# Attention with bias on one core: five landing places instead of four, fewer E tiles and output buffers, and a new written-out order

## The chip, the core and the metric

The kernel runs on one core of a Trainium2 chip. The metric is the device time of one execution in microseconds; the median of several executions counts. A profile is one more execution, taken apart by the hardware profiler: its span is the time from the first to the last instruction of the program, and the execution's own time stands beside it.

The engines of the core are called TensorE (PE: matrix products; its weight loads are PEld), VectorE (DVE), ScalarE (ACT), GpSimd (POOL) and SyncE (SP, which only issues DMAs here).

## The reference

Four batches of eight heads, 1024 queries and keys of 64 numbers each, and one bias matrix for all heads:

```python
batch, n_heads, seq_len, head_dim = 4, 8, 1024, 64
scale = 1.0 / np.sqrt(head_dim)
scores = scale * np.matmul(q, k.transpose(0, 1, 3, 2))
scores = scores + bias                       # bias is (1, 1, 1024, 1024)
scores_max = np.max(scores, axis=-1, keepdims=True)
attn = np.exp(scores - scores_max) / (np.sum(np.exp(scores - scores_max), axis=-1, keepdims=True) + 1e-8)
return np.matmul(attn, v).astype(np.float32)
```

All arrays are float32. The kernel leaves the maximum out, since the scores are small.

## The kernel before

**Work.** The 32 heads are taken as 16 pairs. The 1024 queries of a head are cut into 8 chunks of 128, which gives 256 *slots*, one for each head and chunk. A slot's scores are 128 x 1024 numbers, transposed (keys on the partitions). They lie in two of six PSUM banks, so three slots fit (`pl`, three lanes of two banks). The slots run in two groups of 9 and 7 pairs (`GROUPS`); the first slot of each chunk in a lane adds the bias through TensorE, and a later one in the lane is made from the scores that still stand there: one product over 128 rows adds the new head's scores and subtracts those of the head before (arrays `ke`, `qe` for even heads, `ko`, `qo` for odd ones). From slot 54 on, two slots of neighbouring chunks are a couple and are filled with products of 256 columns.

**Order.** The whole program is a list of tokens, `ORDER` (line 17), which `do` (line 607) turns into instructions one after the other. Each engine runs its own instructions in the order of the list; across engines only data and buffers order them. The tokens:

- `F12`, `G12`: TensorE fills the first and the second bank of slot 12 (line 376, and line 373 with the bias).
- `X12`: ScalarE takes exp of both banks of slot 12 into two halves of the ring `E` of 28 halves (line 399). `P` and `Q` split a round of three slots into two exps of three banks.
- `f r s h c l` with a slot number: VectorE makes the exp of that slot itself, in six steps (`d_steps`): `f` (fixed point, reads PSUM and so frees the banks), `r` (claims an *E tile* of VectorE, from the pool `de`, which also takes the landing of V), `s`, `h`, `c`, `l`. 29 of the 256 slots go this way.
- `A12`: eight products of slot 12's weights with V and a column of ones (line 462). A letter `a` or `b` opens a new bank of products in one of two further PSUM banks, which the transposes `T` use too. `SIZES` tells how many slots a bank takes.
- `R3`, `M3`: VectorE's reciprocal of bank 3's sums, and its evacuation, a multiplication into an output buffer `ob` of the pool `op`, followed by the stores of that bank (line 664). `joined` (line 465) puts neighbouring chunks of a head, and equal runs of neighbouring heads, into one store; the stores go through SyncE's queue but for the last.
- `Tk5a`, `Ck5`, `Dk5p0`, `Sk5`, `Nq9`, `V3`: transposes of pair 5's k on TensorE (in PSUM bank `a`), their copy out, the doubling of rows for the even head, a copy that sets the two heads side by side ahead of the transposes, negation of q, and the copy of V to its place, all on VectorE but `T`. From pair 2 on, the rows of k for the next pair's even head are copied by a DMA on SyncE's queue (line 603), from pair 9 on all rows for even heads, and those of q.
- `U`, `L`: one further piece of the loads of `LOADS` (line 564) is asked for; it is issued by GpSimd. With `L` it also waits for the last VectorE instruction ahead of it in the list ("issued beside VectorE's long steps").

**Loads.** `more` (line 583) hands out the pieces in their fixed order. The first 27 entries of `LOADS` are always allowed. Those behind them, the *late loads* from k9 on, are allowed once the pair `LANDS` before has given its landing place free (for V: once all products of the pair nine before are made). Each piece also waits until an earlier one has landed, so that only so many are under way: `BEHIND` lists how many for the first pieces, and behind that a constant holds. k and q land in the pool `land`, with `LANDS` places for each.

## Time and profile before

| | before |
|---|---|
| three timed runs | 223.55, 224.82, 225.61 us; median 224.82 us |
| profiled execution | 223.97 us, its span 222.2 us |
| TensorE, weight loads | 214.5 us (97%), 197.5 us (89%) |
| ScalarE | 211.6 us (95%) |
| VectorE | 203.6 us (92%) |
| GpSimd | 72.0 us (32%) |
| granted TensorE clock | full in all slices |

How to read the lines shown below. A line of a group names the kernel line, the engine, the operation, what it writes and reads (`out<-in`) with partitions x elements, and the count; behind the bar stand the busy time in us, the mean duration of one in ns, and the engine's idle time just before them with what ended it. A line of the timeline has the start in us, the duration in us, and the instructions merged into it; in square brackets stands the idle time before it. A line that begins with an operation and three numbers gives the shortest, median and longest duration in ns, and the first and last start in us. "DMA to landing" is the time from issue to landing in us. A line of windows gives the stretch, its length and each engine's busy time with its count (PE, PEld, DVE, ACT, POOL), the granted clock, the DMA engines' share and GB/s.

### The profile page before, as it was taken

The numbers are of one execution on the slowest core, as the hardware profiler recorded it, in microseconds if no ns is written. First come the engines' busy times: TensorE is split into PE (matmuls) and PEld (weight loads), VectorE is DVE, ScalarE is ACT, GpSimd is POOL, SyncE is SP. The second block draws the span as 40 slices with busy tenths as digits, with TensorE's granted clock in tenths as the row PEclk, the third lists the DMA queues.
The fourth block names the chain that finished last, engine by engine and source line by source line (L and its number), as shares of the span: only waits on it lengthen the run. The fifth ranks groups of instructions, "written<-read, shape, count | busy, mean of one in ns | idle before, by whom it ended". The sixth has DMA issues, their size and how long they took to land.

```text
span 222.2 us, 9043 instructions
## 1 busy us (share of the span) xinstructions
PE 214.5 (97%) x3965; PEld 197.5 (89%) x3965; DVE 203.6 (92%) x354; ACT 211.6 (95%) x229; POOL 72.0 (32%) x90
## 2 busy tenths in 40 slices
PE   7799999999999999999999999999999999999993
PEld 2689999999999999999998998898988999899992
DVE  2679999999999999999999999989998999999993
ACT  2799999999999999999999999999999999999992
POOL 8824446637464563030635675410000000000000
PEclk9999999999999999999999999999999999999999
DMA  6999999999999999297899999992111112011213
GB/s 174 227 205 216 227 236 146 173 168 190 128 169 164 88 119 166 62 91 176 102 227 204 215 144 190 119 194 57 44 43 33 55 45 66 7 44 44 86 46 106
DMA packets 86327, 28.87 MB, mean 130 GB/s; under 512 B 66384, under 2 KB 83024, under 8 KB 86288
## 3 DMA queue, kind: packets, MB, share of 16 engines
q0 software_dynamic: 62880, 14.06, 69.9%
q1 hardware_dynamic: 22704, 13.44, 22.6%
q10 hardware_dynamic: 704, 0.79, 1.3%
q8 instruction: 31, 0.51, 1.0%
q14 instruction: 8, 0.07, 0.1%
HBM read 29.36 MB, written 8.39 MB: 170 GB/s over the span
## 4 chain that ended last, share of the span: by engine, by line
ACT 78%; PE 17%; DMA 2%; DVE 1%; issue 0%; SPq 0%; DVEq 0%
ACT E L399 78%; PE pl L376 9%; PE po L462 4%; DMA dy<-in_k_dram 2%; PE px L276 2%; PE pl L373 1%; PE px L282 0%; DVE ob L85 0%; DVE de L85 0%; SPq L501 0%; DVE ko L85 0%; PE pl L276 0%; DVE rs L85 0%; DVEq L85 0%
## 5 line engine op out<-in xcount | busy, mean ns | idle before, releaser
L399 ACT ACTIVATE E<-pl 128x1024 bf16<-128x1024 f32 (+2 forms) x225 | 208.7, 1110 | 1.7 <-PE pl L376 1.6
L462 PE MATMUL po<-vall,E 128*128 128x65 bf16 x1816 | 86.9, 194 | 0.4 <-DVE ob L85 0.2
L462 PEld LDWEIGHTS <-E 128*128 128x128 bf16 x1816 | 77.3, 98 | 3.0 <-DVE ob L85 0.4
L376 PE MATMUL pl<-qo,ko 128*128 128x128 bf16 (+1 forms) x752 | 77.9, 239 | 0.6
L376 PE MATMUL pl<-qe,ke 128*128 128x128 bf16 (+1 forms) x648 | 67.2, 239 | 0.5 <-DVE qe L85 0.2
L376 PEld LDWEIGHTS <-ko 128*128 128x128 bf16 x856 | 57.4, 98 | 6.0 <-ACT E L399 2.1
L376 PEld LDWEIGHTS <-ke 128*128 128x128 bf16 x648 | 43.4, 98 | 5.1 <-ACT E L399 2.2
L85 DVE TENSOR_SCALAR dy<-pl 128x1024 int32<-128x1024 f32 x29 | 35.4, 1221 | 3.7 <-PE pl L376 3.4
L85 DVE SCALAR_TENSOR_TENSOR de<-dy,ds 128x1024 uint16<-128x1024 int32 x29 | 35.1, 1217 | 0.2
L213 POOL DMA_DIRECT2D q<-in_q_dram x18 | 16.6, 921 | 23.8 <-DVE de L85 8.8
L213 POOL DMA_DIRECT2D k<-in_k_dram x18 | 15.9, 887 | 24.1 <-DVE q L85 10.2
L85 DVE TENSOR_TENSOR ob<-po,rs 128x448 f32<-128x448 f32 (+3 forms) x38 | 22.7, 600 | 0.4
L250 POOL DMA_DIRECT2D vall<-in_v_dram x18 | 17.9, 996 | 11.9 <-DVE de L85 4.2
L85 DVE TENSOR_SCALAR de<-dy 128x1024 f16<-128x1024 uint16 x29 | 19.8, 695 | 0.1
L85 DVE TENSOR_TENSOR ds<-de 128x1024 f16<-128x1024 f16 x29 | 19.5, 674 | 0.2
L85 DVE TENSOR_TENSOR ds<-ds,de 128x1024 f16<-128x1024 f16 x29 | 19.5, 679 | 0.0
L373 PE MATMUL pl<-ident,braw 128*128 128x128 bf16 x136 | 14.0, 227 | 0.0
L85 DVE TENSOR_SCALAR qo<-px,sgn 128x1024 bf16<-128x1024 bf16 (+2 forms) x18 | 12.3, 684 | 0.7 <-PE px L276 0.7
L85 DVE TENSOR_SCALAR de<-de 128x1024 f16<-128x1024 f16 x29 | 12.6, 444 | 0.1
L462 PE MATMUL po<-vall,de 128*128 128x65 bf16 x232 | 12.5, 194 | 0.0
L373 PEld LDWEIGHTS <-braw 128*128 128x128 bf16 x136 | 11.8, 148 | 0.4
L85 DVE COPY ko<-px 128x1024 bf16<-128x1024 bf16 (+1 forms) x16 | 10.7, 669 | 1.0 <-PE px L282 1.0
(54 smaller groups left out, 126.0 us busy)
## 6 DMA issues: line engine op xcount, KB each, us to landing
ke<-ko SPq DMA_DIRECT2D x20, 128.0 KB, 4.7
k<-in_k_dram POOLq DMA_DIRECT2D x18, 128.0 KB, 5.3
q<-in_q_dram POOLq DMA_DIRECT2D x18, 128.0 KB, 4.8
out_dram<-ob SPq DMA_DIRECT2D x24, 96.0 KB, 2.8
vall<-in_v_dram POOLq DMA_DIRECT2D x18, 128.0 KB, 6.0
out_dram<-ob SPq DMA_DIRECT2D x30, 64.0 KB, 2.2
braw<-in_bias_dram POOLq DMA_DIRECT2D x7, 256.0 KB, 6.2
de<-in_v_dram POOLq DMA_DIRECT2D x7, 256.0 KB, 7.5
```

Of the source, the lines that this page charges most:

```text
L85: i = getattr(self.engine, name)(*args, **kwargs)
L213: return nc.gpsimd.dma_start(out=t[:, :, y, :], in_=(qf, kf)[x][pr][:, y].rearrange("p (c d) -> p c d", d=D))
L250: return nc.gpsimd.dma_start(out=vall[:, (2 * pr + t) % VR, :, :D], in_=vf[pr][:, t])
L276: m = nc.tensor.transpose(px[:, c, :], raws[pr, which, c0][:, c].rearrange("p t d -> p (t d)"), ident[:])
L373: m = nc.tensor.matmul(to, braw[:, c1, :].rearrange("p (kp kc) -> p kc kp", kc=NCH)[:, kc, :], ident8[:], start=i == 0 and order[0] == "b" ...
L376: m = nc.tensor.matmul(pl[:, 2 * x + b, i * P:(i + n) * P], kk[:, kc, :], qq[:, c:c + n, :].rearrange("p c q -> p (c q)"), start=i == 0 an ...
L399: read(nc.scalar.activation(E[:, e0:e0 + n].rearrange("p b x -> p (b x)"), pl[:, b0:b0 + n].rearrange("p b x -> p (b x)"), ACTF.Exp, scale ...
L462: nc.tensor.matmul(bank[b][:, banks[b].index(s), :], weights(s, kc), vall[:, slots[s][2] % VR, kc, :], start=first and kc == 0, stop=kc == ...
```

## The change

The number of landing places for k and for q goes from four to five (`LANDS`), and the constant number of late loads under way from four to five. To make room, VectorE's E tiles go from seven to six and the output buffers from four to three. `ORDER` and `SIZES` are new. Both lists hold the same fills, exps, vector steps, products, transposes, copies and asks for loads, in another order; the letters for banks and the banks' members differ. In the new list the asks for early loads stand spread over the list's first part instead of all at its head. The transposes of pair 0's last q chunks (`Tr0b`) stand ahead of the copy `Sr0` in the new list, so they read the landed q itself, two products for each chunk.

```diff
 ORDER = """
...
-G29 A18 F30 R2 Dk6p0 G30 X29 F31 M2 Tq6b V4 G31 X30 F32 Cq6 G32 A20a f32 X31 A21 F33 G33 Tk7b X33 F34 G34 Dq6p0 Dq6p1
...
-G194 A186 X194 F195 M25 G195 F199 R26 G199 X195 F197 f199 G197 A182a A193 X197 F198 G198 F202 f198 G202 F200 X202 G200
...
-X254 A231 A252 A251 X255 A254a R36 A246 M36 A253 A255 R37 M37
...
+Cq5 U G25 Dq5p1 F25 A14 V3 X23 Dq5p0 F26 G26 X24 U A15 X25 G27 F27 f26 U Sk6 A20 R2 X27 r26 G28 F28 G29 F29 Tk6b G30
+F30 X28 X29 F31 M2 G31 A18a A19 X30 F32 G32 Ck6 X31 Sq6 A22 F33 Dk6p0 V4 G33 X33 U L Tq6b f32 G34 F34 Cq6 Dq6p0 F35
...
+X189 X188 G193 A183 A184 F192 G192 X193 G191 F191 A187 l173 A186 X191 G196 F196 A164 X192 M25 F194 G194 A185a F195
+f196 G195 G199 F199 r196 R26 X194 X195 F197 G197 A188 F198 G198 X197 f199 F202 G202 F200 G200 M26 f198 A197 X202 F201
...
+M34 A248 A247 A249 A231 F253 h246 G253 Q250 c246 X253 A245 A240b R35 l246 F254 G254 A251 F255 G255 A243 A252 X254 M35
+A250 A246 A253a A254 R36 M36 X255 A255 R37 M37
 """
-SIZES = (6, 7, 7, 7, 7, 7, 6, 4, 7, 7, 7, 7, 7, 7, 7, 7, 7, 7, 7, 7, 7, 7, 7, 7, 7, 7, 7, 7, 7, 5, 7, 7, 7, 7, 7, 7,
-         7, 4)
+SIZES = (6, 7, 6, 7, 7, 6, 7, 7, 7, 7, 7, 6, 7, 7, 7, 7, 7, 6, 7, 7, 7, 7, 7, 7, 7, 7, 7, 7, 7, 7, 7, 7, 7, 7, 7, 7,
+         6, 3)
...
-    LANDS = 4
+    LANDS = 5
...
-    op = ctx.enter_context(tc.tile_pool(name="op", bufs=4))
+    op = ctx.enter_context(tc.tile_pool(name="op", bufs=3))
...
-    de = ctx.enter_context(tc.tile_pool(name="de", bufs=7))
+    de = ctx.enter_context(tc.tile_pool(name="de", bufs=6))
...
-                j = i - (BEHIND[i] if i < len(BEHIND) else 4)
+                j = i - (BEHIND[i] if i < len(BEHIND) else 5)
```

More of the change, by code (lines that the diff above doesn't have):

```diff
@@ L23 @@
-F24 X23 G24 Dk5p0 F25 G25 Dq5p0 A17 X24 Dq5p1 F26 G26 Sk6 A14 f26 X25 F27 G27 Tk6b X27 F28 G28 Sq6 A19 X28 Ck6 r26 F29
-G29 A18 F30 R2 Dk6p0 G30 X29 F31 M2 Tq6b V4 G31 X30 F32 Cq6 G32 A20a f32 X31 A21 F33 G33 Tk7b X33 F34 G34 Dq6p0 Dq6p1
-A23 Ck7 X34 F35 G35 A28 s26 F36 X35 G36 Dk7p0 F37 G37 Tq7b X36 A27 Cq7 A22 A29 X37 F38 V5 G38 F39 R3 Dq7p0 G39 X38
-A25b h26 F40 M3 G40 A34 X39 c26 A24 F41 A30 Dq7p1 X40 A31 l26 G41 Tk8a X41 F42 F43 Ck8 G42 G43 X42 A26 f43 F44 G44
-Tq8a X44 F45 Cq8 G45 F46 X45 A33 G46 Dk8p0 F47 A35a Dq8p0 V6 X46 G47 F48 R4 G48 M4 A41 X47 F49 Sr0 G49 f48 A40 A36 X49
@@ L38 @@
-R13 X101 M13 G102 F103 Nq9 L G103 A96b X102 Ck9 L F104 G104 A101 f104 A97 X103 F105 G105 Tk10a X105 l83 F106 G106 F107
-G107 X106 F108 f107 G108 A80 A100 X108 F109 G109 Ck10 A99 X109 F110 G110 r107 A95 F111 X110 R14 G111 M14 A98a F112
-A106 r104 X111 G112 Tq10b A103 X112 Cq10 F113 G113 A109 F114 Nq10 X113 G114 s107 Tq11b F115 X114 Cq11 G115 F116 G116
-h107 L A108 X115 F117 f116 L U G117 Tk12b X117 F118 G118 Ck12 A105 A102 X118 F120 R15 G120 s104 Tk11b X120 F121 M15
-G121 F119 Ck11 L G119 X121 F123 G123 f119 A83a A112 X123 F124 G124 Tq12b c107 X124 F122 Cq12 G122 F126 A110 X122 l107
@@ new lines @@
+F71 R7 M7 A58 G73 X69 l48 F73 X71 A66 F72 G72 A64 X72 h43 X73 h59 A69a F74 G74 c43 F75 G75 A61 X75 c59 G76 F76 A67 f74
+A65 X76 F77 R8 G77 A63 A71 M8 l59 G79 F79 G78 X77 X79 F78 l43 A73 G80 F80 A59b G82 F82 R9 f80 X78 A75 A76 G81 F81 X82
+F83 G83 r68 G85 f83 r74 X81 F85 A78 A72 F84 G84 A70 X85 X84 F86 G86 F88 A48 G88 M9 X86 G87 F87 A84a r80 A79 F89 A85
+s80 R10 X87 s68 A86 M10 G89 s74 h68 X88 h80 F90 G90 X89 c68 G91 F91 F92 X90 X91 h74 G92 G93 F93 A81 A77 F94 l68 X92
+A91b R11 A82 c74 G94 Dq8p1 X93 G95 A89 A87 F95 F96 X94 G96 M11 X95 A93 Tq9a G97 X96 F97 X97 r83 c80 A92 A90 G98 Cq9
@@ new lines @@
+F98 R12 G99 M12 X98 Nq9 Tk9a F99 G100 F100 A95b A32 U U G101 F101 X99 l74 A88 Ck9 G102 F102 A97 X100 A100 F103 A98 A74
+s83 l80 R13 X101 X102 L G103 M13 F104 X103 G104 f104 A94a F105 G105 Tk10b G106 F106 G107 F107 X105 X106 h83 Ck10 G108
+F108 U L f107 U A102 A80 G109 F109 A105 X108 X109 G110 F110 Tq10b F111 X110 G111 G112 F112 X111 r104 A96 c83 A43 s104
+Cq10 r107 X112 F113 A99 R14 G113 G114 M14 s107 h104 Tq11b F114 X113 A101a Cq11 A103 G115 X114 F115 A108 Nq10 G116 F116
+F117 L G117 Tk12b X115 X117 f116 L L L F118 G118 Ck12 L A106 F119 X118 G120 F120 Tk11b X120 F121 G121 G119 A114 X121
@@ new lines @@
+l196 X210 A207a G209 G213 F213 A196 A201 r203 G212 F212 F209 X213 s199 X212 A195 X209 G215 F215 h199 X215 F214 c199
+A211 G214 s203 X214 G216 c198 F216 G218 X216 F218 A155 A204 R28 F217 G217 M28 G219 X218 F219 X217 A216b l198 F221 G221
+h203 l199 X221 f219 A213 F220 G220 X220 r219 c203 R29 G222 F222 A206 G224 X222 F224 f224 A212 F223 G223 A210 G225 F225
+X223 F227 A221 G226 X225 F226 P226 M29 A220 G227 r224 F228 G228 A215a A209 A214 A222 F229 A173 G229 Q226 X229 F230
+s219 s224 h219 A217 h224 R30 F231 G230 A199 M30 X230 G231 F232 G232 X232 A198b F233 G233 l203 c224 f231 R31 X233 r231
@@ new lines @@
+A218 M31 F234 G234 F235 G235 A225 F236 G236 X234 f235 F237 G237 X236 A227 l224 F238 F239 G238 A223 X237 A224 G240 G239
+c219 r235 F240 l219 P238 A228 A229a A226 F241 R32 Q238 s235 F242 G241 h235 A237 A219 G243 P241 G242 F243 A234 A232
+A238 M32 G244 c235 F244 Q241 X244 s231 R33 A230b F245 A233 l235 h231 F246 G245 G246 A241 G247 F247 f246 X245 A236 A235
+G248 c231 F248 r246 M33 F249 A203 X247 G249 G250 F250 X248 A244 l231 X249 F251 R34 A239a A242 G251 s246 F252 P250 G252
+M34 A248 A247 A249 A231 F253 h246 G253 Q250 c246 X253 A245 A240b R35 l246 F254 G254 A251 F255 G255 A243 A252 X254 M35
```

73 lines of the change are left out of this document (30 added, 43 removed).

## The prediction

> **What bounds the kernel now.** I began with the page: busy time, the DMA row of the slices, and the chain of waits.
>
> ```profile
> span 222.2 us, 9043 instructions
> PE 214.5 (97%) x3965; PEld 197.5 (89%) x3965; DVE 203.6 (92%) x354; ACT 211.6 (95%) x229; POOL 72.0 (32%) x90
> DMA  6999999999999999297899999992111112011213
> ACT 78%; PE 17%; DMA 2%; DVE 1%; issue 0%; SPq 0%; DVEq 0%
> ```
>
> Three engines are busy for over 90% of the span and the chain runs on ScalarE for 78% of it. The DMA engines are full until slice 28 (about 155 us) and nearly idle behind it. So the next question is how much ScalarE loses, from its groups kept apart by shape, its timeline and its waits.
>
> ```profile
> L399 ACT ACTIVATE E<-pl 128x1024 bf16<-128x1024 f32 x213 | 196.5, 1104 | 0.9 <-PE pl L376 0.9
> L399 ACT ACTIVATE E<-pl 128x1536 bf16<-128x1536 f32 x8 | 11.3, 1529 | 0.0
> L399 ACT ACTIVATE E<-pl 128x512 bf16<-128x512 f32 x4 | 2.2, 598 | 0.9 <-PE pl L376 0.8
> ...
> 8.34 4.10 ACT L399 ACTIVATE E<-pl 128x512 bf16<-128x512 f32 x6 [0.77 <-PE pl L376]
> 12.70 24.85 ACT L399 ACTIVATE E<-pl 128x1024 bf16<-128x1024 f32 x27 [0.26 <-PE pl L376]
> 37.84 2.85 ACT L399 ACTIVATE E<-pl 128x1024 bf16<-128x1024 f32 x3 [0.29 <-PE pl L376]
> 99.38 13.01 ACT L399 ACTIVATE E<-pl 128x1024 bf16<-128x1024 f32 x14
> 172.30 45.71 ACT L399 ACTIVATE E<-pl 128x1024 bf16<-128x1024 f32 x46 [0.32 <-PE pl L376]
> ```
>
> The exps overlap: 14 of them take 13.01 us, of which the last one's own duration is 1.10, so 13 starts lie 11.91 us apart, 0.916 us each. At that pace 213 exps are 195.1 us; with the 11.3 and 2.2 of the other shapes 208.6. From the first exp (8.34) to the end of the last (172.30 + 45.71 = 218.01) are 209.67 us. ScalarE thus loses **1.07 us** in all between its first and last exp; its three waits there, 0.26, 0.29 and 0.32, make 0.87 of it. No order of the same exps gains more than 1.07 us, save at the head and the tail.
>
> The profiled execution took 223.97 us, 1.77 more than its span. The three timed runs have a median of 224.82 (223.55 to 225.61), so the profiled one stands 0.85 under the median and inside their spread. I put the sum on the middle of the two, 224.4. One per cent of the median is 2.25 us: under 222.57 is faster, over 227.07 slower, about what a measurement of this kernel can tell from no change.
>
> **The change part by part.** Computation: both lists hold the same tokens up to the letters for PSUM banks; the same 29 slots go to VectorE, and ScalarE's exps have the same shapes. The sizes of the banks sum to 256 in 38 banks as before, so evacuations cost the same. The last bank shrinks from four outputs to three.
>
> ```profile
> 218.53 0.18 DVE L85 RECIPROCAL rs<-po 128x4 f32<-128x4 f32 x1 [0.45 <-PE po L462]
> 218.75 0.42 DVE L85 TENSOR_TENSOR ob<-po,rs 128x256 f32<-128x256 f32 x1
> L85 DVE TENSOR_TENSOR ob<-po,rs x38: 416/618/626, 20.7 to 218.7; 128x448 f32<-128x448 f32 x33, 128x384 f32<-128x384 f32 x2, 128x256 f32<-128x256 f32 x2, 128x320 f32<-128x320 f32 x1
> ```
>
> Seven outputs take 0.618, four 0.42: 0.066 an output, so three save **0.07 us**, and on the path. As before, only A255 stands behind the last exp.
>
> *Order.* I took ScalarE's three waits one by one. At 12.70 each engine's tokens up to X2 stand in the same order in both lists: 0.26 stays. The one at 37.84 is VectorE's lateness:
>
> ```profile
> 33.62 0.42 DVE L85 COPY side<-q 128x1024 bf16<-128x1024 bf16 x1
> 33.96 0.68 DVE L85 COPY ko<-px 128x1024 bf16<-128x1024 bf16 x1
> ...
> 35.65 0.43 DVE L85 COPY ke<-ko 64x1024 bf16<-64x1024 bf16 x1
> 36.01 0.60 DVE L85 TENSOR_TENSOR ob<-po,rs 128x448 f32<-128x448 f32 x1
> ...
> 36.67 0.69 PE L462 MATMUL po<-vall,E 128*128 128x65 bf16 x16 [0.22 <-DVE ob L85]
> ```
>
> TensorE waits 0.22 us for evacuation M2 to open the next bank (A20), and ScalarE starves behind it. The new list puts Sq6, Ck6 and Dk6p0 (0.42 + 0.68 + 0.43 = 1.53 us) behind M2 instead of before it, but also opens the bank one exp (0.92) earlier: M2 is 0.6 us better placed, against 0.22 wanted. I take this loss as gone: the exp starts 25.14 us after the one at 12.70, where 27 at the pace are 24.73, so **0.41 us**; if something else takes the place, 0.
>
> The third wait is a pattern at slots 199 to 202:
>
> ```profile
> 170.37 1.22 DVE L85 TENSOR_SCALAR dy<-pl 128x1024 int32<-128x1024 f32 x1 [0.35 <-PE pl L376]
> 171.65 0.61 PE L376 MATMUL pl<-qo,ko 128*128 128x256 bf16 x4
> 172.10 0.41 PE L373 MATMUL pl<-ident,braw 128*128 128x128 bf16 x4
> 172.34 0.39 PE L376 MATMUL pl<-qs,ko 128*128 128x128 bf16 x4
> ```
>
> VectorE's f199 empties a pair of PSUM banks until 171.59, F202 and G202 fill it from 171.65 (0.45 to the next start), and X202 follows at 172.30. Both lists have G199, f199, F202, G202, X202 in this order, with X194, X195 and X197 between. The 0.32 stays; 0 to 0.2 is possible where fewer value products stand around it. Elsewhere I summed, over the lists, the filling between each exp that frees banks and the exp that needs them: the tightest place is this one in both.
>
> *Five landing places and five late loads under way.* These touch the loads from k9 on.
>
> ```profile
> 95.37 1.74 POOL L213 DMA_DIRECT2D k<-in_k_dram  x2 [10.25 <-DVE q L85]
> 115.68 0.87 POOL L213 DMA_DIRECT2D q<-in_q_dram  x1 [0.67 <-DVE q L85]
> DMA to landing us min/median/max: 3.9/5.3/6.8
> 124.16 0.61 PE L276 MATMUL px<-ident,q 128*128 128x128 bf16 x8
> ```
>
> The third line is for loads issued between 110 and 130 us. k13 waits 10 us at GpSimd for a landing place, but that wait is not ScalarE's. The tightest late load is q14's second half: issued at 115.68, landed at 119.6 to 122.5, used at 124.16, so even then 1.7 us early. The change asks for it at the list's place of f116, about 10 exps earlier, and uses it 6 us later. What was hidden gets better hidden: **0**. For v13 to v15 the new list allows the loads only once pair 4's products are made (pairs 5 and 6 by the same place), 5.5 us later than v13 before; uses lie 11 us behind that, against landings of up to 6.8 plus a few issues of 0.87. Cover remains, some 3 us.
>
> *Loads beside VectorE's steps.* Twelve of the 42 late load pieces now stand within five tokens of the vector step that gates them, against 27 before; other gates are long past when the piece goes.
>
> ```profile
> L85 DVE TENSOR_SCALAR de<-de x29: 373/419/786, 42.9 to 212.5; 128x1024 f16<-128x1024 f16 x29
> 60.00:160.00 100.00, 99.59 (x1834) 92.67 (x1831) 95.39 (x154) 100.00 (x111) 38.30 (x42) 1.00 1.23 142
> ```
>
> A vector step beside a load's issue was stretched at worst from 0.419 to 0.786, by 0.37 us. Fifteen more ungated pieces cost VectorE 0 to 15 x 0.37 = 5.5 us in a stretch in which it idles 100 - 95.39 = 4.6: 0 to 0.9 on the path. I take 0, since the median step, 0.419, lies near the minimum. The Trainium skill, "SBUF — State Buffer", section "Who interferes with whom", says that a vector copy in a two-port mode and GpSimd lock each other out for a whole instruction; the trace agrees in direction, and by that rule alone the end of 0.9 would be the likelier.
>
> *Six E tiles for seven.* By the list at most five are alive when another is claimed, and the claim that comes soonest behind the release it needs (r203, r235) has four exps, 3.7 us, between. Cost 0; a late value product would have to be four exps late.
>
> *Output stores and three buffers.* Adjoining outputs of a head leave in one store. Working them out from both lists, the new banks hold outputs that join less: 164 stores for 116, all but one on SyncE's queue.
>
> ```profile
> L664 SPq DMA_DIRECT2D out_dram<-ob x113: 332/431/2031, 21.3 to 219.2; - x113
> 84.01 13.14 SPq L664 DMA_DIRECT2D out_dram<-ob  x14
> DMA to landing us min/median/max: 1.5/3.3/6.3
> ...
> DMA to landing us min/median/max: 1.5/1.6/2.8
> ...
> DMA to landing us min/median/max: 3.3/5.2/6.0
> ```
>
> The landings are those of stores issued from 76 to 98 us, of stores from 205 to 217, and of the ke copies from 14 to 50. SyncE's extra issues are 48 x 0.431 = 20.7 us, off the path. What counts is an evacuation that must wait until the stores of three banks ago have landed: behind it on VectorE stand the next step that empties score banks, and TensorE waits for the bank of products. In the list M13 stands 15 exps (13.8 us) behind M10. M9 and M10, two exps apart, now have 7 and 6 stores: 13 x 0.431 + 3.3 - 1.8 = 7.1 us behind M10, 6.7 us to spare. From M34's start to M37's stand a wide exp (11.3 / 8 = 1.41), three exps (2.75), the last one's overlap (0.19), product (0.45) and reciprocal (0.2): 5.0 us, 4.4 from M34's end. Its four stores need 4 x 0.421 (the median of those from 205 us on, taken as 0.431) + 1.6 = 3.3: 1.1 to spare. The copies of k to ke also queue behind stores: Ck6's behind M2's four, issued about 38.3 us (M2's end, 36.6, and 4 x 0.431), landed by 44.3 at the slowest, for F42 at 44.8 by the exps ahead of it. Cost **0**; uncovered up to 0.5 here, more in the rival below. The Trainium skill, "DMA: Bandwidth & Descriptors", section "Specifications", says that transfers under 512 B fall below line rate. The rows of an output are 256 B, and the single ones grow from 55 to 145; no row here separates their landing by size.
>
> Sum: -0.41 - 0.07 = -0.48 us, with bounds of -1.14 (all ScalarE's losses and the tail) and +1.4 (0.9 and 0.5). On 224.4 that is **223.9 us**.
>
> **The rivals.** *All losses go* (the waits at 12.70 and 172.30 too, or early loads that came late in the slower timed runs now meet later uses): 224.4 - 1.14 = 223.3, and on the profiled run 222.8. For it: V and S steps up to q6 mostly stand one or two exps later in the list. Against it: the first and third wait are the same chains. Chance 0.16, of which 0.07 under 222.57, by scatter.
>
> *The stores take the path*: slower. If an issue takes what the 14 stores from 84.01 took on end, 13.14 / 14 = 0.94, and landings the slowest of their window, M13 is 13 x 0.94 + 6.3 - 1.8 - 13.8 = 2.9 us late, less about 0.5 that the filled banks hold; M37 is 4 x 0.94 + 2.8 - 4.4 = 2.2 late, with nothing behind it. 223.9 + 2.4 + 2.2 = 228.5. It decides from an issue of 0.95 at the median landing, or 0.72 at the slowest. For it: SyncE's slowest issue, 2.03, and full DMA engines. Against: the median of 0.431, and quiet engines at the end. Chance 0.12, 0.10 of it over 227.07.
>
> *The loss only moves*, with VectorE stretched by the ungated loads and ke copies late: 224.4 + 0 to 1.4, about 225.2. For: VectorE at 95% of its time. Chance 0.14, 0.02 of it slower. In this case the larger landing area does nothing.
>
> **How the numbers follow.** Forecast 0.58. Range: from the floor on the profiled run, 222.8, to the third rival's end with half a microsecond of scatter, 226.3; that leaves out the stores' rival and little else. Faster 0.07, same 0.81, slower 0.12.
>
> **What would show it.** ScalarE's timeline should keep waits near 12.7 and 172 us and have none near 37.8. GpSimd's 10 us wait for k13 should be gone and the time not show it. SyncE should issue some 160 stores; VectorE's waits should name no output store before an ob step. Wrong it would be if ScalarE's idle time rose over 2 us, if ob waited for DMA, or if the 0.916 pace changed.

## The result, and the profile after

| | before | after |
|---|---|---|
| median (20 executions each) | 223.81 us (222.94 to 225.61) | 225.94 us (224.32 to 227.50) |
| ratio | | 1.008, 95% interval 1.0057 to 1.0102 |
| profiled execution, its span | 223.97 us, 222.2 us | 225.71 us, 223.9 us |

The change makes the kernel slower by 0.8%, 2.1 us, where I forecast 0.5 us off. The time lies inside my range, and within 1%; the forecast and its direction were wrong. Here and below, medians and ratios leave out an execution that took over 1.5% more than its kernel's fastest: one of a_lands4 and one of a_de7 (with them 226.29 and 225.79 us), and one of before. The page after, in the order of the prediction: span, busy time, the DMA row of the slices, the chain by engine and by line.

```profile
span 223.9 us, 9114 instructions
...
PE 214.2 (96%) x3970; PEld 197.5 (88%) x3970; DVE 204.5 (91%) x354; ACT 212.3 (95%) x229; POOL 71.2 (32%) x90
...
DMA  6999999999999992299999999993111111121133
...
PE 46%; DVE 19%; DMA 14%; ACT 11%; issue 4%; SPq 3%; DVEq 0%
PE pl L376 27%; PE po L462 13%; DMA out_dram<-ob 12%; ACT E L399 11%; DVE de L85 6%; PE px L276 5%; DVE ob L85 4%; SPq L664 3%; DVE dy L85 3%; DMA dy<-in_k_dram 2%; DVE ds L85 2%; PE pl L373 1%; DVE ko L85 1%; DVE qe L85 1%; DVE rs L85 1%
```

The chain left ScalarE (78% before, 11% now), and 12% of it are output stores (all DMAs made 2% before). ScalarE's timeline after:

```profile
12.72 141.22 ACT L399 ACTIVATE E<-pl 128x1024 bf16<-128x1024 f32 x153 [0.34 <-PE pl L376]
154.28 18.66 ACT L399 ACTIVATE E<-pl 128x1024 bf16<-128x1024 f32 x20 [0.34 <-PE pl L376]
173.26 45.71 ACT L399 ACTIVATE E<-pl 128x1024 bf16<-128x1024 f32 x46 [0.32 <-PE pl L376]
```

The waits at 12.7 and at slot 202 stayed, the one at 37.84 us did not show, a new one stands at 154.28. The last exp ends at 173.26 + 45.71 = 218.97, which is 0.96 later than before; the span ends 4.89 us behind it instead of 4.20. So 0.96 us were lost under the exps, and 0.69 in the tail. The tail first: VectorE's timeline and the chain of waits, in order of time, both of after.

```profile
219.49 0.18 DVE L85 RECIPROCAL rs<-po 128x3 f32<-128x3 f32 x1 [0.22 <-PE po L462]
220.50 0.36 DVE L85 TENSOR_TENSOR ob<-po,rs 128x192 f32<-128x192 f32 x1 [0.83 <-DMA out_dram<-ob]
```

```profile
216.26 0.43 SPq L664
216.69 0.04 issue
216.74 3.64 DMA out_dram<-ob
```

M37, the last evacuation, waited 0.83 us for M34's fourth store, which was issued at 216.74 and landed 3.64 us later. That is the place that I had priced with "1.1 to spare". In the records of this store 15 of its 16 parts had landed by 218.32, the last one 2.06 us later. In the same time a 16-KB block of TensorE's instructions was on its way (218.23 to 219.19).

Under the exps the losses are small and many. I measured, for each exp, by how much its end stands further behind the end of the one before than at ScalarE's pace. In the execution that was profiled: 0.23 us at 53 to 56 us, 0.34 at 98 to 106, 0.16 at 115, and 0.67 at 154. Together with 0.08 before 50 us that is 1.48 us; against it stands what the profile of before lost at 37.84 us and behind it and this one did not, 0.52, and so the last exp is 0.96 later. The loss at 154 is TensorE's, which stood still for 0.52 us with all its inputs there:

```profile
152.67 0.68 PE L462 MATMUL po<-vall,E 128*128 128x65 bf16 x16
153.86 0.82 PE L376 MATMUL pl<-qo,ko 128*128 128x256 bf16 x10 [0.52 <-issue]
```

The executions scatter more than before: of the 20 after, 12 took over 225.6 us, up to 227.5; before, one of 20, at 225.61. A single trace can't tell that; the experiments had to.

### The profile page after: what moved, and what is told of

It is laid out like the page before. It is cut to its first block, busy times and chain, and to the rows that moved or that the text cites. A ratio compares the mean times of both kernels' runs of the same rounds, so it can differ in the third digit from the quotient of the medians.

```text
span 223.9 us, 9114 instructions
## 1 busy us (share of the span) xinstructions
PE 214.2 (96%) x3970; PEld 197.5 (88%) x3970; DVE 204.5 (91%) x354; ACT 212.3 (95%) x229; POOL 71.2 (32%) x90
## 4 chain that ended last, share of the span: by engine, by line
PE 46%; DVE 19%; DMA 14%; ACT 11%; issue 4%; SPq 3%; DVEq 0%
PE pl L376 27%; PE po L462 13%; DMA out_dram<-ob 12%; ACT E L399 11%; DVE de L85 6%; PE px L276 5%; DVE ob L85 4%; SPq L664 3%; DVE dy L85 3%; DMA dy<-in_k_dram 2%; DVE ds L85 2%; PE pl L373 1%; DVE ko L85 1%; DVE qe L85 1%; DVE rs L85 1%
## 5 line engine op out<-in xcount | busy, mean ns | idle before, releaser
L85 DVE TENSOR_TENSOR ob<-po,rs 128x448 f32<-128x448 f32 (+2 forms) x38 | 22.9, 601 | 1.9 <-DMA out_dram<-ob 1.4
L250 POOL DMA_DIRECT2D vall<-in_v_dram x18 | 17.1, 953 | 19.2 <-PE po L462 15.8
L462 PE MATMUL po<-vall,de 128*128 128x65 bf16 x232 | 12.7, 194 | 0.0
```

Source lines behind the costliest of these rows:

```text
L85: i = getattr(self.engine, name)(*args, **kwargs)
L250: return nc.gpsimd.dma_start(out=vall[:, (2 * pr + t) % VR, :, :D], in_=vf[pr][:, t])
L462: nc.tensor.matmul(bank[b][:, banks[b].index(s), :], weights(s, kc), vall[:, slots[s][2] % VR, kc, :], start=first and kc == 0, stop=kc == ...
```

## The experiments

All ratios are to the kernel before, which ran with each set. "Lands, loads, E, buffers" are the landing places, late loads under way, E tiles and output buffers; before has 4, 4, 7, 4 and the changed kernel 5, 5, 6, 3. The sets ran on different chips, and before took 223.8 to 224.7 us in them, so across sets the ratios are compared and not the medians.

| run | order | lands, loads, E, buffers | executions | median us | ratio (95%) |
|---|---|---|---|---|---|
| changed kernel | new | 5, 5, 6, 3 | 20 | 225.94 | 1.0080 (1.0057 to 1.0102) |
| a_again | new | 5, 5, 6, 3 | 6 | 226.88 | 1.0103 (1.0054 to 1.0153) |
| a_behind4 | new | 5, 4, 6, 3 | 6 | 225.71 | 1.0078 (1.0051 to 1.0105) |
| a_lands4 | new | 4, 5, 6, 3 | 5 | 226.09 | 1.0090 (1.0054 to 1.0125) |
| a_de7 | new | 4, 5, 7, 3 | 8 | 225.60 | 1.0070 (1.0042 to 1.0098) |
| a_l4op3 | new | 4, 4, 7, 3 | 9 | 224.98 | 1.0043 (1.0022 to 1.0064) |
| a_de6 | new | 4, 4, 6, 4 | 12 | 224.85 | 1.0045 (1.0018 to 1.0073) |
| a_pools | new | 4, 4, 7, 4 | 12 | 224.42 | 1.0025 (1.0001 to 1.0048) |
| b_pools | old | 5, 5, 6, 3 | 12 | 223.75 | 0.9995 (0.9974 to 1.0017) |

### The same kernel again

> The changed kernel once more, word for word, to see what of its trace comes back. Every theory expects a ratio of 1.008 to the kernel before (225.7 us). Theory A (the evacuations meet the stores of three output buffers): the last evacuation waits again for M34's stores, 0.5 to 0.9 us, and the span's end stands 0.6 to 0.8 us later behind the last exp than before. Theory C (the loads bunched by five under way make TensorE's instructions arrive late): TensorE stands dry again for about 0.5 us near 153.5 us and ScalarE loses 0.6 us there. If one of the two does not come back while the time does, it is not what makes the kernel slower.

The loss at 154 us did not come back; those at 53 (0.21), 98 to 106 (0.35) and 115 us (0.16) did, to within 0.02. M37 waited again, 0.48 us, as it did, by 0.29 to 1.17 us, in all nine profiles of the new order in which it draws on three buffers and TensorE's instructions were not shifted (see below). This execution took 224.73 us, the others of the run up to 227.82. So there is a part that both profiles show, and one that an execution may pay or not.

### The end of the run

> The changed kernel with a fourth buffer for the last evacuation alone (its three outputs, 768 bytes), so M37 waits for no store. Theory A in its simple form (the wait is the loss): 0.8 us come back, 225.0 us, ratio 1.004. Theory A': SyncE's queue is as late as the wait was: M36's second store, issued at 220.6 us in the changed kernel and landed at 222.4, ends the run instead of M37's (222.7), so only 0.2 us come back, 225.5 us, ratio 1.007. Theory C: the same 0.2 to 0.8 us of the tail at most, with the loss near 154 us as before. M37's wait for the output stores must be gone under all.

```diff
-    olast = consts.tile([P, 1, D], F32)
+    olast = consts.tile([P, 3, D], F32)
-        ob = olast if n == 1 and last else op.tile([P, 7, D], F32, name="ob")
+        ob = olast if last else op.tile([P, 7, D], F32, name="ob")
```

225.72 us, ratio 1.0073 (1.0038 to 1.0107). M37's wait went, and the run was hardly faster: M36's two stores left SyncE's queue at 221.21 and 221.64 in the profiled execution, 1.2 and 1.6 us behind the end of the last exp (220.06), and landed last, at 223.4 and 223.5; M37's landed at 223.2.

> As the run before it, and the last exp is put ahead of M36 in the written order, so that M36's two stores leave from ScalarE's queue, behind the last exp, as they did in the kernel before (one of them). Theory A': now 0.9 to 1.1 us come back (the last store issued near 220.1 us, M35's at 219.6 landing at 221.4 us), 224.8 us, ratio 1.004, and the tail behind the last exp is as short as before, 4.0 to 4.2 us. If the wait alone was the loss, this is no faster than the run with the buffer alone. The rest, 0.9 us and more, stays under theory C until the loads are put back.

```diff
-A250 A246 A253a A254 R36 M36 X255 A255 R37 M37
+A250 A246 A253a A254 R36 X255 M36 A255 R37 M37
```

225.09 us, 1.0057 (1.003 to 1.0084): the tail behind the last exp was 4.29 us, nearly the 4.20 of before. That fits theory A': the wait and the queue lay side by side, and only both together give time back. It is about 0.5 us by the ratios, half of what was expected, and the intervals overlap; the tail of one profile doesn't prove it either, for a_gated below, whose last stores are the changed kernel's, had 4.29 us too (M37 waited 0.34 us there).

> The changed kernel's order with all places put back (224.42 us) and the last exp ahead of M36 in the written order, so that M36's stores leave from ScalarE's queue. All theories: the last stores leave 0.3 to 0.4 us earlier, 224.1 us, ratio 1.000 to 1.002. If this is no faster than 224.4 us, the end of the run is not set by SyncE's queue there.

The same two tokens exchanged in a_pools. 224.58 us, 1.005 (1.0022 to 1.0079), no faster than a_pools, although the tail of its profile went from 4.64 to 4.29 us. Five of its 12 executions took over 225.6 us: the part that comes by chance hides 0.35 us.

### Why the store was late

> The changed kernel with its ten warm-up matmuls of 512 columns at the start cut into 80 of 64 columns, so that TensorE's instruction stream is 140 instructions longer ahead of the first transpose and every 16-KB block of instructions is asked for some 3.5 us earlier in the program: the last block at 213.8 to 214.8 us instead of 217.4 to 218.2. Theory F (an instruction block on its way holds one of the DMA engines, and a store that has a part there lands 1 to 2 us late): M34's third and fourth store land within 1.5 us of their issue instead of 3.4 to 4.0, M37 waits for no store, and the tail behind the last exp shrinks from 4.6 to 4.9 us to 4.2 to 4.4, so 0.3 to 0.6 us come back: 225.3 to 225.6 us. If the stores are as late as before, the lateness is not the blocks'. The block near 151 us moves too, to about 147 us, where more stores and loads are on their way: the loss near 154 us may come more often, and hide the gain in the median.

```diff
-        for i in range(10):
-            wrote(nc.tensor.matmul(pl[:, 4, :], zeros[:, :P], zeros, start=True, stop=True), 4)
+        for i in range(80):
+            wrote(nc.tensor.matmul(pl[:, 4, :64], zeros[:, :P], zeros[:, :64], start=True, stop=True), 4)
```

The last block of instructions was now on its way from 213.89 to 215.47 us. M34's third and fourth store, issued at 216.38 and 216.86, landed 1.7 and 1.6 us later, M37 did not wait, and the tail was 4.32 us. VectorE's timeline:

```profile
218.80 0.18 DVE L85 RECIPROCAL rs<-po 128x3 f32<-128x3 f32 x1 [0.22 <-PE po L462]
219.02 0.36 DVE L85 TENSOR_TENSOR ob<-po,rs 128x192 f32<-128x192 f32 x1
```

In their place M33's stores, issued at 212.55 to 213.57 beside the block, were late: 3.1 to 3.6 us to landing. The lateness goes with the block; theory F holds. The median, 225.99 us (1.0075), does not show the gain: in half of the executions the time outside the span grew by up to 1 us, and the part that comes by chance was there.

### Order and places apart

> The changed kernel's order and bank sizes with the kernel before's places: four landing places, four late loads under way, seven E tiles, four output buffers. Theory C: the five loads are what jams the transfers, so the loss near 154 us and the late instruction fetch of 151 us go, -0.6 us; with the fourth buffer -0.2 to -0.8 us at the end: 224.4 to 225.0 us, ratio 1.002 to 1.005. Theory A: only the end, 225.0 to 225.5 us, ratio 1.004 to 1.007. Theory D (the written order alone is the slower one, the places do nothing): as the changed kernel, 225.9 us, ratio 1.008. An order written for five places can also be slower with four, if a load comes late: then VectorE or TensorE waits for a transfer between 100 and 160 us, and the run tells nothing of theory C.

```diff
-    LANDS = 5
+    LANDS = 4
-    op = ctx.enter_context(tc.tile_pool(name="op", bufs=3))
+    op = ctx.enter_context(tc.tile_pool(name="op", bufs=4))
-    de = ctx.enter_context(tc.tile_pool(name="de", bufs=6))
+    de = ctx.enter_context(tc.tile_pool(name="de", bufs=7))
-                j = i - (BEHIND[i] if i < len(BEHIND) else 5)
+                j = i - (BEHIND[i] if i < len(BEHIND) else 4)
```

224.42 us: about 70% of the loss came back with the places, and the intervals are apart. What stays, 0.25%, is the order's own, its interval barely clear of 1. The opposite run:

> The kernel before with the changed kernel's places alone: five landing places, five late loads under way, six E tiles, three output buffers; its order and gates stay. Theory A: the three buffers cost at the end and wherever an evacuation meets stores, +0.3 to +0.8 us, 224.2 to 224.7 us. Theory P: the gates still hold the loads beside VectorE's long steps, so the loads cost nothing; in this order the evacuations stand at least 7 us behind the stores of their buffer up to M35, so 223.8 to 224.2 us. Theory D (order and places belong together, either one alone is worse): over 224.7 us.

The same four lines the other way, in the kernel before. 223.75 us, no difference. The small places cost nothing where the order does not lean on them. Theory P was closest to that.

> The changed kernel's order with four landing places, four late loads under way and seven E tiles, as in the run that put all places back (224.42 us), but with three output buffers. Theory A (the three buffers are what costs): the wait of M12 near 91 us and the late steps behind it (ScalarE loses 0.35 us between 98 and 106 us) come back, and with them the wait at the end of the run: 225.2 to 225.8 us. Theory P (it is the loads: a load that POOL issues beside one of VectorE's short steps stretches that step by up to 0.4 us, and at 97.0 us it is the load that the fifth landing place lets go): M12 may wait, but ScalarE loses nothing between 98 and 106 us; only the end costs 0 to 0.7 us: 224.4 to 225.1 us.

As a_pools with `bufs=3` for `op`. 224.98 us, 0.2% above a_pools by the ratios (0.4 us), and the intervals overlap. In the two profiles the difference lies under the exps: the last exp ends at 218.47 instead of 218.00, and the tails are alike, 4.65 and 4.64 us, although M37 waited:

```profile
219.88 0.36 DVE L85 TENSOR_TENSOR ob<-po,rs 128x192 f32<-128x192 f32 x1 [0.71 <-DMA out_dram<-ob]
```

And M12 waited 0.53 us, as in every kernel with three buffers in this order. VectorE's timeline of the changed kernel:

```profile
90.17 0.20 DVE L85 RECIPROCAL rs<-po 128x7 f32<-128x7 f32 x1 [0.20 <-PE po L462]
90.90 0.62 DVE L85 TENSOR_TENSOR ob<-po,rs 128x448 f32<-128x448 f32 x1 [0.53 <-DMA out_dram<-ob]
```

The profile names a store, but M9's seven stores had landed by 84.4 us. What stands there are four wait instructions at 90.18, 90.25, 90.34 and 90.44 us, for seven semaphores, and then 0.41 us for which I have no cause. In a_pools, with M8's six stores and three wait instructions, the same step waited 0.10 us. With this wait alone (a_l4op3) ScalarE lost 0.21 us between 98 and 106 us, with the changed kernel's loads 0.34, in a_pools nothing.

> The changed kernel with one thing put back: four late loads under way instead of five (from k9 on); five landing places, six E tiles and three output buffers stay. Theory C (the five loads jam the transfers, near 140 to 153 us above all, so that TensorE's instructions come late in some executions): the loss of 0.7 us near 154 us does not show, the executions of 226.8 us and more become rare, the median is 225.0 to 225.4 us. Theory L (the fifth landing place and what it lets go early is the cause, not their number under way): no change, 225.6 to 226.8 us.

The constant 5 of `BEHIND` is 4 again. 225.71 us.

> The changed kernel with the other thing put back: four landing places instead of five; five loads under way, six E tiles and three output buffers stay. Theory L: the load that was let go at 96.9 us and stretched VectorE's step at 97.15 us (0.42 to 0.85 us) comes later, ScalarE's loss of 0.18 us at 100.4 us goes, and the long executions become rare: median 224.9 to 225.3 us, as the run with three buffers and everything else put back (224.98). Theory C: no change but that 0.2 us: 225.6 to 226.7 us.

`LANDS = 4` alone. 226.09 us. Neither of the two alone brings anything in the median: theories C and L both fall as single causes. In the traces the piece that each forecast did go. The loss of 0.18 us near 100.4 us stands in all nine profiles with the fifth landing place in the new order, and in none of the six without. TensorE's stop near 154 us stands in five of the ten profiles of the new order with five loads under way, and in none of the five with four; the last section has its times. As far as these traces go, each place adds a piece of its own.

> The changed kernel's order with four landing places, five late loads under way, three output buffers and seven E tiles: one E tile more than the run with four landing places (226.29 us), and one load more under way than the run with three output buffers and the rest put back (224.98). If the six E tiles are what opens the way to the long executions: 224.8 to 225.2 us. If the five loads under way are: 225.8 to 226.5 us, and the trace of a long execution shows more of VectorE's short steps stretched between 50 and 80 us. If neither alone is, but chance in where the loads fall, it lies between.

As a_lands4 with `bufs=7` for `de`. 225.60 us, between the two forecasts.

> The changed kernel's order with four landing places, four late loads under way and four output buffers (all put back, 224.42 us) except for six E tiles. If the six E tiles are the cause of the long executions: 225.2 us and more, half of the executions over 225.4. If not: 224.4 to 224.6 us, as with seven.

As a_pools with `bufs=6` for `de`. 224.85 us, 0.4 above a_pools, with four of 12 executions over 225.4 instead of one. The intervals overlap. What the table bears is that all places together cost 0.5% in the new order and nothing in the old one. That the three buffers make up about a third of it is what a_l4op3 suggests, within overlapping intervals; how the rest is shared between landing places, loads under way and E tiles stays open.

### The part that comes by chance

What did the long executions have? The profiled one of a_olast took 226.58 us. GpSimd's issues and VectorE's steps in it, from the two timelines:

```profile
38.56 0.87 POOL L213 DMA_DIRECT2D q<-in_q_dram  x1 [0.24 <-DMA q<-in_q_dram]
40.41 0.87 POOL L213 DMA_DIRECT2D q<-in_q_dram  x1 [0.98 <-DMA de<-in_v_dram]
41.27 0.72 POOL L246 DMA_DIRECT2D de<-in_v_dram  x1
```

```profile
38.85 0.81 DVE L85 TENSOR_SCALAR qe<-qo 64x1024 bf16<-64x1024 bf16 x1
...
40.78 0.72 DVE L85 TENSOR_SCALAR de<-de 128x1024 f16<-128x1024 f16 x1
41.54 0.70 DVE L85 TENSOR_SCALAR qe<-qo 64x1024 bf16<-64x1024 bf16 x1
```

In a_again, the short execution, the same three steps:

```profile
38.79 0.42 DVE L85 TENSOR_SCALAR qe<-qo 64x1024 bf16<-64x1024 bf16 x1
...
40.34 0.41 DVE L85 TENSOR_SCALAR de<-de 128x1024 f16<-128x1024 f16 x1
40.78 0.42 DVE L85 TENSOR_SCALAR qe<-qo 64x1024 bf16<-64x1024 bf16 x1
```

Three steps of 0.42 us took 0.81, 0.72 and 0.70, each beside a load that GpSimd issued, and behind them a_olast's ScalarE starved:

```profile
45.40 1.94 ACT L399 ACTIVATE E<-pl 128x1024 bf16<-128x1024 f32 x2 [0.36 <-PE pl L376]
47.71 6.72 ACT L399 ACTIVATE E<-pl 128x1024 bf16<-128x1024 f32 x7 [0.37 <-PE pl L376]
```

The loads of this stage go when an earlier one lands, at times that differ by some tenths from execution to execution, so which step is hit differs too. Over all traces, behind 13 us, each VectorE step that took over 60 ns more than its form does otherwise stood beside a GpSimd issue. Summed from 26 to 50 us and from 50 to 80 us, with what ScalarE lost there (us; one profiled execution each):

```
kernel         26-50: stretched  lost    50-80: stretched  lost
before                    1.24   0.52              0.52    0.04
b_pools                   1.07   0.38              0.77    0.04
b_ungated                 0.99   0.26              0.97    0.00
b_dummy                   0.89   0.00              0.53    0.00
b_dummy8                  1.47   0.00              0.62    0.21
a_l4op3                   0.27   0.00              0.78    0.49
a_pools                   0.45   0.00              0.69    0.31
a_gated                   0.64   0.00              0.14    0.20
a_tail                    0.47   0.08              0.43    0.24
a_dummy                   0.57   0.09              0.41    0.31
a_again                   0.77   0.06              0.93    0.27
changed kernel            0.80   0.08              0.30    0.26
a_de7                     0.87   0.14              0.45    0.54
a_pools_tail              0.99   0.33              0.55    0.33
a_shift                   1.11   0.00              0.37    0.40
a_de6                     1.66   1.14              0.38    0.18
a_lands4                  1.68   0.72              1.56    1.22
a_dummy8                  1.82   0.89              0.89    0.88
a_olast                   1.90   1.19              1.22    1.00
a_behind4                 2.12   1.38              0.29    0.21
```

In the stage from 26 to 50 us ScalarE lost nearly all of what the stretching came to beyond some 0.7 us, in most rows; a_shift (1.11) and b_dummy8 (1.47) lost nothing, so the sum alone does not decide. In this stage the new order is not stretched more than the old one (1.07 us in the mean of its 15 profiles, 1.13 in the old order's five); it scatters more, and lost 0.41 us in the mean against 0.23. Between 50 and 80 us the old order took up 0.5 to 1 us for 0.2 us or less, and the new one lost 0.2 to 1.2. Of that about 0.2 us, at 53 to 56 us, are the order's own: a_gated lost them with no stretched step there, and their cause was not traced. That the old order takes up more in this stage fits what VectorE waited for TensorE's scores in the whole run, its own slack: the two rows are of before and of a_again.

```profile
DVE dy L85 <- PE pl L376: 3.4, 9, 0.5
```

```profile
DVE dy L85 <- PE pl L376: 1.0, 4, 0.4
```

This is a comparison of traces, not an experiment. The experiments on it:

> The kernel before with one part of the change alone: of the 16 late loads k9 to q12, the ten that were gated behind a step of VectorE are let go as soon as a load under way allows it; places, buffers and order stay. Theory P: these loads now fall on VectorE's short steps by chance, so the median rises by 0.4 to 1.2 us (224.3 to 225.1) and the executions spread more (before: half of them within 0.6 us). Theory A: nothing changes, 223.9 us, ratio 1.000 +- 0.002. If four landing places hold the loads back anyhow, the effect is smaller and the trace shows POOL waiting for the places.

```diff
-A54b R6 L U r59 G62 F63 A49 L M6 X62
+A54b R6 U U r59 G62 F63 A49 U M6 X62
...
-A79 h74 L F89 G89 h68 L U A77 X88
+A79 h74 U F89 G89 h68 U U A77 X88
```

Ten of the asks, from k9 to q12, become free. 224.04 us, 1.0011 (0.9991 to 1.003): theory P expected 0.4 us or more, so it failed here. The stretched sum of the stage did rise (0.52 to 0.97 us), and the old order took it up.

> The changed kernel with the 16 late loads k9 to q12 gated again, each behind the VectorE step ahead of a long one (the first or last step of an exponential of VectorE's, or an evacuation), where they were let go freely between 58 and 77 us; the rest is the changed kernel's. Theory P: the executions that take 226.8 us and more become rare and the median falls by 0.5 to 1.0 us, to 225.0 to 225.5 us; the loss of 0.35 us between 98 and 106 us and the tail stay. Theory A: no change, 225.9 to 226.9 us. If the long executions come from the loads between 26 and 45 us instead, which this leaves as they are, there is no change either, and the trace of a long one shows stretched steps there.

```diff
-A44 Dr1p0 L f59 r59 s43 s48 G60 X58 F60 U A45 A46
+A44 Dr1p0 L f59 r59 s43 s48 G60 X58 F60 A45 A46
...
-F71 R7 M7 A58 G73
+F71 R7 L M7 A58 G73
```

The 16 asks of k9 to q12 stand ahead of f59, M6, l32, f68, M7, l48, f74, M8, l59, l43, f80, f83, M9, M10, l68 and M11. 225.47 us, 1.0064 (1.0039 to 1.0089): 0.5 less in the median than the changed kernel, inside the intervals; five of 12 executions still took over 225.5. In the profiled execution the stage from 50 to 80 us was clean (0.14 us stretched). That execution was a short one (224.46 us), so it doesn't tell where the long ones of this run come from; the stage before, which this run leaves alone, and TensorE's stop near 154 us are left.

> The changed kernel with twelve small loads more (128 partitions of two rows of 32 bytes, into a tile that nobody reads), issued by POOL between 155 and 212 us, where the changed kernel has no load, each let go by the VectorE step two before a shift of VectorE's exponential, so that POOL issues it beside that step (0.42 us). Theory P: ten or more of the twelve shifts take 0.75 to 0.85 us, 4 to 5 us more of VectorE's time in all; VectorE stands idle for 1.0 to 1.6 us between 150 and 215 us, so ScalarE's loss there rises by 2.5 to 3.5 us: 228.5 to 229.5 us. If POOL's issue does not hold VectorE (the stretched steps of the other runs came from something that only went with it, as the transfers themselves), the shifts stay at 0.42 us and the time at 225.9.

```diff
+                if kind == "h" and s in beside_h:
+                    extra = nc.gpsimd.dma_start(out=spare[:, beside_h.index(s)], in_=qf[0][:, :, :8])
+                    tc.add_manual_dep(extra.ins, vec.prior.name, DATA, reason="beside a short step")
                 chain[s].pop(0)()
```

`vec.prior` is the VectorE step before the last one recorded.

> The kernel before with the same twelve small loads beside the same twelve shifts. Theory P: the shifts take 0.75 to 0.85 us here too, 4 to 5 us in all; VectorE is idle for 2.1 us between 150 and 215 us in this order, so the loss is 1 us smaller than in the changed kernel: 1.5 to 2.5 us, 225.4 to 226.4 us, ratio 1.007 to 1.011. If the kernel before loses as much as the changed one, VectorE's idle time is no measure of what an order can take up. If POOL's issue does not hold VectorE: 223.9 us.

225.74 us, 1.0103 (1.0057 to 1.0149), and 224.52 us, 1.0013 (0.9988 to 1.0038): no measurable cost, and the expectation failed. Only two shifts of 12 in the new order and four in the old one were clearly stretched, to between 0.58 and 0.65 us. But they were the only steps behind 146 us that were stretched by over 60 ns, in these or any trace without loads there, and all six began 0.29 to 0.34 us behind the start of GpSimd's issue. Nine others that began 0.01 to 0.22 us behind it, and lay wholly inside it, took their 0.42. So it is GpSimd's issue that does it, and only in its second part. The six ended alike: a step's start and its stretch together came to 0.50 to 0.52 us behind the start of the issue each time. So they were not slowed; they stood still until then. (The changed kernel's run with these loads had four executions.)

> As the run of the changed kernel with twelve small loads more, but each load is one of 128 partitions of eight pieces (1024 descriptors, as many as a real k, q or V load has, instead of 256), so that POOL's issue takes 0.87 to 1.0 us instead of 0.70. There only two of the twelve shifts were stretched (0.60 and 0.64 us for 0.42), both of those that began 0.29 to 0.34 us behind the start of POOL's issue; those that began less than 0.23 us behind it were not. Theory P, refined (POOL holds VectorE's short steps in the second part of its issue, while it writes the descriptors, and that part grows with their number): eight or more of the twelve shifts take 0.55 to 0.85 us, 2 to 4 us in all, and ScalarE's loss between 150 and 215 us rises by 1 to 3 us: 227 to 229 us. If a stretch of 2 us or more does not reach ScalarE, VectorE's stretching is not what makes the long executions long.

> The kernel before with the same twelve loads of eight pieces. Theory P: eight or more of the shifts are stretched as in the changed kernel, 2 to 4 us in all. If the order of before takes up more, because VectorE is idle for 2.1 us instead of 1.0 to 1.6 between 150 and 215 us, the loss is at least 0.5 us smaller for the same stretch: 224.5 to 226 us. If the orders differ only in how often a load falls on a short step, the loss for the same stretch is the same.

```diff
-in_=qf[0][:, :, :8])
+in_=qf[0][:, 0].rearrange("p (c d) -> p c d", d=D)[:, :, :8])
```

With as many pieces as a real load: GpSimd's issue and VectorE's step in a_dummy8, from the two timelines.

```profile
207.62 0.88 POOL L672 DMA_DIRECT2D spare<-in_q_dram  x1 [9.28 <-DVE rs L85]
```

```profile
207.91 0.80 DVE L85 TENSOR_SCALAR de<-de 128x1024 f16<-128x1024 f16 x1
```

228.0 us, 1.0159 (1.0093 to 1.0226, four executions), and 224.5 us, 1.0005 (0.9977 to 1.0033). Four shifts were stretched in the new order (1.5 us in all), three in the old one (0.9), not eight; the step shown above was held until 0.68 us behind the issue's start (0.29 and the 0.38 that it took over its 0.42, before rounding). Behind these steps ScalarE lost 0.57 and 0.22 us, where the profiles without added loads lose nothing: the stretch does reach it, by four tenths and a quarter. That differs too little to say that the old order takes up more in this stage; most of the 228 us came from earlier (1.8 us lost between 26 and 80 us in the profile, 0.44 at TensorE's stop near 155 us).

## Why the prediction was wrong, by its own steps

The steps that failed are the two terms that I put at 0, the loads beside VectorE's steps and the output stores with three buffers, and under them the reading that the new order costs nothing by itself. The runs showed 0.8% in all: the order alone 0.25%, and the places, which cost nothing in the old order, the rest.

- **The base.** I put the sum on 224.4, the middle of the profile and three runs. Twenty executions gave 223.81; 0.6 of the miss is not in the change's costs at all. The floor was misread too: in "1.07 us in all" the 11.3 and 2.2 are durations that overlap. By the ends of the exps ScalarE lost 1.5 us before, so the bounds were 0.5 too narrow.
- **The last bank, -0.07.** M37 took 0.36 instead of 0.42: right.
- **The wait at 37.84, -0.41.** It was gone in the profile after (0.08 lost there), but not for my reason. b_ungated has the order of before up to there, and no wait there. In VectorE's lines that I showed for M2's lateness, the line under the first "..." was this one of before:

```profile
34.56 1.07 DVE L85 TENSOR_SCALAR de<-dy 128x1024 f16<-128x1024 uint16 x1
```

  The step is otherwise 0.68: 0.39 us beside a load's issue, more than the 0.22 that TensorE then waited for M2. In b_pools, the same order, the wait was there again, with 0.15 us and another stretched step, the copy of k's rows ahead of M2 (0.67 for 0.41); in b_ungated, b_dummy and b_dummy8 it was not. I took a collision for a property of the order, and counted its absence as a gain.
- **The waits at 12.7 and at slot 202 stay.** Right, 0.34 and 0.32.
- **Five landing places, 0.** GpSimd no longer waits for a place, but k13's second half waited 18.13 us for its gate, a reciprocal of VectorE, so "k13's wait gone" was wrong. With that gate q13's first half goes at 96.90 and hits a short step:

```profile
96.03 0.87 POOL L213 DMA_DIRECT2D k<-in_k_dram  x1 [18.13 <-DVE rs L85]
96.90 0.87 POOL L213 DMA_DIRECT2D q<-in_q_dram  x1
```

```profile
97.15 0.85 DVE L85 TENSOR_SCALAR de<-de 128x1024 f16<-128x1024 f16 x1
```

  In a_pools, where q13 goes at 99.0 us, this step takes 0.42. ScalarE's loss of 0.18 at 100.4 us comes with it in all nine profiles with the fifth landing place in the new order, and in none of the others.
- **Loads beside VectorE's steps, 0 (0 to 0.9).** I took 0 because the median step lay near the minimum; but a median says nothing of a cost that a few steps pay, and VectorE's idle time in a window, which I set against it, is no credit where the next score banks hang on the stretched step. I also looked at the late loads alone. The early ones, from 26 to 45 us, cost most where they struck: 1.1 to 1.4 us in three of the profiles of the new order, but in the mean of all profiles 0.41 against 0.23 in the old order. No run shows how much of the median is theirs. The Trainium skill, "SBUF — State Buffer", section "Who interferes with whom", has the two engines lock each other out for a whole instruction, which I set aside; its direction was right, and these runs show such a full stop for a part of the issue: 0.42 becomes 0.86 at most, and a step begun in the first 0.2 us isn't held.
- **Six E tiles, 0.** In the old order 0. In the new one a_de6 against a_pools shows 0.4 us with overlapping intervals; open.
- **Output stores.** 164 and "6.7 to spare" for M13 were right, and M12 lost 0.53 us for another reason, of which its wait instructions explain a part. For M37 the time from M34's end to its need was 4.5 us (I had 4.4), but the stores took 5.2 and not 3.3: SyncE was still busy with M33's, and the last landing took 3.64 us where I had put the median of 1.6. The row that I quoted had 2.8 as its maximum, and the slack of 1.1 did not cover it together with a queue. It came back in all nine profiles with three buffers (0.29 to 1.17 us). What I had not seen is that M36's stores now stand ahead of the last exp in the list and so on SyncE's queue.

Of the rivals, *the loss only moves* (225.2, chance 0.14) names what happened, with a small piece of *the stores take the path* at the end. What both profiles of the changed kernel lost beyond before is 0.2 us at 53 us, 0.5 between 98 and 115 us, and 0.69 and 0.35 in the tail, which was shorter still in other kernels with the same last stores (0.1 in a_gated): together 1.0 to 1.4 us. The rest of the 2.1 us is the part that comes by chance, of which the traces show the held steps and, in five of them, TensorE's stop near 154 us; how it divides in the median stays open. That the kernel happened to lie inside my range is no credit to the sum: two of its terms at 0 were wrong, and its one gain had another cause.

## What to carry to other kernels

A stall in one profile belongs to the order only if it comes back in a second one: look for a step on the path that took longer than its form does elsewhere, and for what another engine issued beside it. Price a buffer by the slowest landing and by the queue ahead of the store, not by the median landing; a resource that can be shrunk for nothing in one order may be what the next order leans on. Taking away one of two waits that lie side by side, as here a buffer and a queue, gives next to nothing.

## What the runs showed of the hardware that I had not expected

- **TensorE's instructions share the DMA engines.** The page's row for the queue of instructions has 31 packets (0.51 MB) in 223.9 us: blocks of 16,384 bytes, one for about 256 instructions of TensorE (7,935 matmuls and weight loads in 31 blocks), 0.9 to 1.9 us each. Of 151 stores and copies on SyncE's and ScalarE's queues before, 23 had a last part that landed over 0.8 us behind the fifteenth, of 199 after 26; each was under way beside such a block (of TensorE's, or of another engine's in the next queue). Most stores beside a block were not late.
- **TensorE stops when such a block comes late.** The stop of 0.52 us in the profile after came where a block began 11.1 us, and some 430 of TensorE's instructions, behind the one before, and arrived at 152.4 us. At the same place TensorE stopped in four more profiles; two of them, a_de7 and a_lands4:

```profile
153.64 0.82 PE L376 MATMUL pl<-qo,ko 128*128 128x256 bf16 x10 [0.41 <-issue]
```

```profile
156.80 0.83 PE L376 MATMUL pl<-qo,ko 128*128 128x256 bf16 x10 [0.57 <-issue]
```

  Set against the exp that starts three before the delayed one, the block arrived 1.25 to 1.66 us later in these five, and ScalarE lost 0.42 to 0.72 us there, more the later it came but for one pair. In the nine other profiles of the new order with the same stream it arrived at most 0.88 us later and no such stop shows. In a_shift, where the blocks lie 140 instructions elsewhere, TensorE did not stop here. This is a comparison of traces, and no run moved this block alone; why it is late more often with five loads under way was not tested.
- **GpSimd's issue of a load holds VectorE's short steps, but only in the later part of the issue.** Over all 20 profiles, behind 13 us, 213 steps of up to 0.45 us (copies, casts and products with a constant) began in the first 0.2 us of an issue, and none was stretched. Beside issues of 0.87 to 0.89 us 109 began 0.23 to 0.61 us behind the start, and all were: start and stretch together came to 0.68 to 0.70 us each time, so a step stood still until some 0.19 us before the issue's end. (Beside issues of 0.70 that point is 0.50 to 0.55.) That is why 0.42 becomes 0.86 at most. The other way round it is GpSimd that waits: of 125 issues of k and q with such a step under way 0.23 to 0.28 us behind their start 91 took over 0.92 us, of 537 with no step of these kinds under way there 4. Steps of 1.22 us and products of two tensors (0.68) were not stretched in any trace.
- **A wait for seven stores, all long landed, cost VectorE 0.53 us**, of which four wait instructions stand for a part; 0.41 us are unexplained.
